# A two-block fp32 model on one core: the second block's causal masks moved from TensorE to VectorE, its factor matmuls spread over more rows, its output gates through tanh, and four pooled tiles held back instead of two

## Chip, core and metric

The kernel runs on one core of one Trainium2 chip. The metric is device time in microseconds (us), from the first to the last instruction; the median of three runs counts.

## The reference, cut to what matters

A first block (dilated attention, convolution, recurrence, feed-forward; width 1024, 1024 tokens) is followed by two layers of a second block over 16 meta tokens and the 1024. The change touches the second block only:

```python
for l in range(2):
    u_pool, z_pool, c_q, c_kv, k_rope, z_mla, g_pool, g_mla = split(rmsnorm(h) @ w_in[l])
    y_pool = (pool_mix(u_pool) * silu(z_pool)) @ pool_w_up[l]
    # 8 heads, q and k of 96, rms-normed per head and token
    s = q @ k.T / sqrt(96);  s = where(key <= query, s, -1e30)
    o = softmax(s) @ v
    y_mla = (o * silu(z_mla)) @ mla_w_up[l]
    merged = sigmoid(g_pool) * y_pool + sigmoid(g_mla) * y_mla
    h = h + merged @ w_out[l]
```

## The kernel before

Everything lies transposed, channels on the 128 partitions and tokens along a row (L2 = 1040). Each fp32 operand is split into a high and a low part, and each product is three matmuls (`mm3`, lines 125 to 127: wh by xh, wh by xl, wl by xh). A row of tokens is cut into chunks: 352, 344, 344 in layer 0, 512 and 512 in layer 1, whose last layer leaves the meta tokens out. A framework schedules the program when it is built: each engine executes its own fixed list in order and waits on semaphores for the others.

Per layer, `attn2` is the middle of the work. For each of eight heads `prep` multiplies q and k by their norm factors: `frh` holds the factors as rows (high parts in rows 0 to 24, low parts in 32 to 56), and a matmul with the selector `esel` (`fp`, line 1535) repeats them over the head's rows. Then it finds each query's largest score: a matmul per query tile of 128 and key chunk of up to 512 (`mx`, line 1552); where the tile's diagonal lies in the chunk, a second matmul adds a bf16 mask through the identity (line 1554); VectorE reduces the bank to a column (line 1555). The negated maxima go into row 96 of q.

The scores proper stand transposed, keys on partitions: `st` (lines 1592 to 1594), on the diagonal again a mask matmul (line 1596), then exp on ScalarE (line 1602), its high part `ph` (1605 or 1607), its low part `pl` (1608) and three matmuls into `ob` (1624 to 1626). `run` issues score tile i and, `LAG` = 3 tiles later, its `ob`. There are 18 score tiles a head in layer 0 and 14 in layer 1. Three PSUM banks rotate for `st`, five for the other products.

Since a head's chain passes through three engines, `run` mixes in other matmuls from `fill`: first the 16 tiles of the two output gates, stored to DRAM, then the eight pooled tiles `mp` (from `th` and `tl`, the split pooled input, line 1291), each multiplied by its gate `gp` (line 1282). `units` counts the pieces of fill and `keep` of them are not handed out before the end of the last head; the rest of `fill` follows at the end of `run`.

At the end the sums `lcol` of the softmax are inverted and copied by DMA into rows of `rh` (high parts from row 0, low parts from row 32; `rlgrp`), and a matmul with the selector `ep` (`rb`, line 1490, in `om_pair`) repeats them over the heads' rows. The last head pair's three (two in layer 1) `rb` can only come after the last `ob`. Then the attention tiles `oh`, `ol` go through `mla_w_up` and are merged under the second gate `gm` (lines 1407 to 1415).

Of the kernel before, what the change touches and what calls it, by code (L numbers as in the profile page):

```python
# [11 lines left out]
F32R = mybir.dt.float32r  # L12
BF = mybir.dt.bfloat16
# [33 lines left out]
def f(t):  # L47
    return t.bitcast(F32)


class B:
# [1010 lines left out]
    def layer(self, l):  # L1062
# [190 lines left out]
        def fill():  # L1253
            for dst, m0 in ((self.gpd[l], 21), (self.gmd[l], 29)):
                for m in range(8):
                    wh, wl = self.w(win[m0 + m])
                    t = self.d("gt")
                    for c0, n in CM:
                        ps = self.mmb()
                        for k in range(8):  # L1260
                            self.mm3(ps[:, :n], [(wh[:, wk(k)], wl[:, wk(k)], xh[k][:, c0:c0 + n], xl[k][:, c0:c0 + n])],
                                     first=k == 0, last=k == 7)
                            if k == 7:
                                nc.vector.tensor_tensor(t[:, c0:c0 + n], ps[:, :n], zs[:, c0:c0 + n], op=OP.mult)
                                if c0 + n == L2:
                                    nc.sync.dma_start(dst[m][:, M0:], t[:, M0:])
                            yield
            for g in range(4):
                t = self.d("tr")
                nc.sync.dma_start(t[:, M0:], self.td[l][g][:, M0:])  # L1270
                h, lo = self.ur("th"), self.ur("tl")
                nc.vector.tensor_copy(h[:, M0:], t[:, M0:])
                nc.vector.tensor_tensor(lo[:, M0:], t[:, M0:], f(h[:, M0:]), op=OP.subtract)
                th.append(h)
                tl.append(lo)
            for m in range(8):
                if m % 2 == 0:
                    wh, wl = self.w(self.i[f"pu_{l}"][m // 2])
                off = 512 * (m % 2)
                t = self.d("gp")  # L1280
                nc.sync.dma_start(t[:, M0:], self.gpd[l][m][:, M0:])
                nc.scalar.activation(t[:, M0:], t[:, M0:], AF.Sigmoid)
                y = mp[m] = self.u("mp")
                for c0, n in CM:
                    ps = self.mmb()
                    for k in range(4):
                        wk4 = slice(off + 128 * k, off + 128 * k + 128)
                        self.mm3(ps[:, :n], [(wh[:, wk4], wl[:, wk4], th[k][:, c0:c0 + n], tl[k][:, c0:c0 + n])],
                                 first=k == 0, last=k == 3)
                        if k == 3:  # L1290
                            nc.vector.tensor_tensor(y[:, c0:c0 + n], ps[:, :n], t[:, c0:c0 + n], op=OP.mult)
                        yield

        silu_gate(17, self.zd[l][0])
# [26 lines left out]
            else:  # L1321
                nc.sync.dma_start(self.qnd[l][m][:, M0:], t[:, M0:])

        fr = self.ur("frh", (57, L2))
        nc.gpsimd.memset(f(fr[0:57, :]), 0.0)

        def qstats():
            if HSD & 1:
                yield YD
            hs.add(0)  # L1330
            if HSD & 2:
                yield YD
            headinv(hs.done(), aq, 16, False)
            for _ in range(HS2):
                yield YD
            for g in range(3):
                ps = self.axb("fr")
                part = T2[4 * g:4 * g + 4]
                for q, (c0, n) in enumerate(part):
                    nc.tensor.transpose(ps[0:25, 128 * q:128 * q + n], FR[:n, 4 * g + q, :], self.ident[:n, :n])  # L1340
                c0 = part[0][0]
                wd = part[-1][0] + part[-1][1] - c0
                nc.scalar.activation(fr[0:25, c0:c0 + wd], ps[0:25, :wd], AF.Copy)
                nc.vector.tensor_tensor(fr[32:57, c0:c0 + wd], ps[0:25, :wd], f(fr[0:25, c0:c0 + wd]), op=OP.subtract)
            yield YD

        att = self.attn2(l, fr, fill())
# [53 lines left out]
        for m in range(8):  # L1401
            if m % 2 == 0:
                wh, wl = self.w(self.i[f"mu_{l}"][m // 2])
            off = 512 * (m % 2)
            t = self.d("gm")
            nc.sync.dma_start(t[:, M0:], self.gmd[l][m][:, M0:])
            nc.scalar.activation(t[:, M0:], t[:, M0:], AF.Sigmoid)
            h, lo = self.ur("gh"), self.ur("gl")
            gh.append(h)
            gl.append(lo)  # L1410
            y = mp[m]

            def ev(ci, c0, n, ps, t=t, y=y, h=h, lo=lo):
                nc.vector.tensor_tensor(t[:, c0:c0 + n], ps, t[:, c0:c0 + n], op=OP.mult)
                nc.vector.tensor_tensor(y[:, c0:c0 + n], y[:, c0:c0 + n], t[:, c0:c0 + n], op=OP.add)
                nc.scalar.activation(h[:, c0:c0 + n], y[:, c0:c0 + n], AF.Copy)
                if late:
                    late.pop(0)()
                late.append(lambda: nc.vector.tensor_tensor(lo[:, c0:c0 + n], y[:, c0:c0 + n], f(h[:, c0:c0 + n]), op=OP.subtract))
            (self.projk if m == 0 else self.proj)(wh, wl, lambda k: slice(off + 128 * k, off + 128 * k + 128), oh, ol, CM, ev)  # L1420
# [38 lines left out]
    def rlgrp(self, l, h0, h1):  # L1459
# [8 lines left out]
        nc.vector.tensor_copy(rlh[R, :nl], rl[R, :nl])  # L1468
        nc.vector.tensor_tensor(rll[R, :nl], rl[R, :nl], f(rlh[R, :nl]), op=OP.subtract)
        rh = self.rh  # L1470
        for q, t in ((0, rlh), (32, rll)):
            for h in range(h0, h1):
                nc.sync.dma_start(f(rh[q + h:q + h + 1, M0:]).rearrange("o (a b) -> o a b", a=16), f(t[16 * h:16 * h + 16, :nl]))

# [24 lines left out]
    def attn2(self, l, fr, fill):  # L1499
# [7 lines left out]
        HT, VT = {}, {}  # L1507
        self.lcol = self.tiny("lcol", (P, 65))
        self.oh, self.ol = [], []
        self.rh = self.ur("rh", (40, L2))  # L1510
        nc.gpsimd.memset(f(self.rh[0:40, :]), 0.0)

        def prep(hd):
            qf, kf = self.d("qf", (96, L2)), self.d("kf", (97, L2))
# [30 lines left out]
            for i, (q0, n) in enumerate(QT):  # L1545
                ke = q0 + n
                for ci, k0 in enumerate(range(0, ke, 512)):
# [1 line left out]
                    ps = self.mmb("mx")  # L1549
                    dg = max(k0, q0)  # L1550
                    has = dg < k1
                    nc.tensor.matmul(ps[:n, :k1 - k0], qh[0:96, q0:q0 + n], kh[0:96, k0:k1], start=True, stop=not has)  # L1552
                    if has:
                        nc.tensor.matmul(ps[:n, dg - k0:k1 - k0], self.idb[:n, :n], self.mk[:n, 1, dg - q0:k1 - q0], start=False, stop=True)  # L1554
                    nc.vector.tensor_reduce(mxp[:n, i, ci:ci + 1], ps[:n, :k1 - k0], axis=AX, op=OP.max)  # L1555
                    yield
            mx = self.tiny("mx2", (P, NT2))
            nc.vector.tensor_reduce(mx, mxp, axis=AX, op=OP.max, negate=True)
# [23 lines left out]
        def s_part(hd, c0, n, j, lastj):  # L1582
# [8 lines left out]
            diag = d1 > s0 and s0 < 128 * j + kn  # L1591
            mms = [lambda: nc.tensor.matmul(st[:kn, :w], kh[0:97, ksl], qh[0:97, s0:c1], start=True, stop=False),  # L1592
                   lambda: nc.tensor.matmul(st[:kn, :w], kh[0:96, ksl], ql[0:96, s0:c1], start=False, stop=False),  # L1593
                   lambda: nc.tensor.matmul(st[:kn, :w], kl[0:96, ksl], qh[0:96, s0:c1], start=False, stop=not diag)]  # L1594
            if diag:
                mms.append(lambda: nc.tensor.matmul(st[:kn, 0:d1 - s0], self.idb[:kn, :kn], self.mk[:kn, 0, s0 - 128 * j:d1 - 128 * j],  # L1596
                                                    start=False, stop=True))

            def evac():
                p = self.s("p")  # L1600
                ph, pl = self.sr("ph"), self.sr("pl")
                nc.scalar.activation(p[:kn, :w], st[:kn, :w], AF.Exp, scale=SC)  # L1602
                state["i"] = i = state.get("i", -1) + 1
                if i % PHD < PHA:
# [37 lines left out]

        def run():
            units = 16 * len(CQ0) * 8 + 8 * len(CQ0) * 4
            keep = 2 * len(CQ0) * 4
            done = 0
            pend = []
            gen = None
# [64 lines left out]
    def b2_consts(self):  # L1713
# [2 lines left out]
        bof = self.tiny("bof", (P, 63))  # L1716
        nc.sync.dma_start(bof, self.i["bo"])
        nc.vector.tensor_copy(self.bo, bof.rearrange("p (a b) -> p a b", a=7))
        self.esel = self.c2p.tile(list((57, 16, 97)), F32R, name="esel")
        ef = self.u("ef", (57, 1024))  # L1720
        nc.sync.dma_start(ef[:, :776], self.i["esel"][:, 0:776])
        nc.vector.tensor_copy(self.esel[:, 0:8, :], ef[:, :776].rearrange("p (a b) -> p a b", a=8))
        ef = self.u("ef", (57, 1024))
        nc.sync.dma_start(ef[:, :776], self.i["esel"][:, 776:1552])
        nc.vector.tensor_copy(self.esel[:, 8:16, :], ef[:, :776].rearrange("p (a b) -> p a b", a=8))
        self.ep = self.c2p.tile(list((40, 4, P)), F32R, name="ep")
        ef = self.u("ef", (40, 512))
        nc.sync.dma_start(ef, self.i["ep"])
        nc.vector.tensor_copy(self.ep, ef.rearrange("p (a b) -> p a b", a=4))

# [8 lines left out]
def _consts():  # L1739
# [39 lines left out]
    bk = np.zeros((128, 9), np.float32)  # L1779
    bk[:32, 8] = 1.0  # L1780
    bo = np.concatenate([bo, bk[:, None]], 1)
    esel = np.zeros((57, 16, 97), np.float32)
    for h in range(8):
        esel[h, h, :64] = 1.0
        esel[8 + h, h, 64:96] = 1.0
        esel[24, h, 96] = 1.0
        esel[16 + h, 8 + h, :96] = 1.0
    esel[32:56] = esel[0:24]
    ep = np.zeros((40, 4, 128), np.float32)
    for m in range(4):  # L1790
        ep[2 * m, m, :64] = 1.0
        ep[2 * m + 1, m, 64:] = 1.0
    ep[32:40] = ep[0:8]
    ic = np.ones((4, 16), np.float32)
    for g in range(4):
        w = 2 << g
        cnt = np.minimum(np.arange(1, 17), w).astype(np.float32)
        ic[g] = np.float32(w) / cnt
    icnt = np.tile(ic.reshape(1, 64), (128, 1))
    return dict(bo=bo.reshape(128, 63), esel=esel.reshape(57, 1552), ep=ep.reshape(40, 512), icnt=icnt, cst=cst, qp=qp, sel1=sel1, e2=e2, mask=mask.reshape(128, 384))  # L1800


def _layout(x):
# [102 lines left out]
```

## Time and profile before

| | |
|---|---|
| median of three runs | 2974.47 us (2971.53 to 2975.08) |
| profiled execution | 2971.57 us, its span 2969.8 us |
| TensorE matmul busy | 2893.7 us, 97% |
| VectorE busy | 1707.3 us, 57% |
| ScalarE busy | 973.8 us, 33% |
| granted TensorE clock | 0.984 of full |

Busy time of TensorE counts from a matmul's start to its modelled end, and matmuls overlap: 97% says that there is nearly always one under way, not how densely they follow each other. That is read from the distance between their starts.

### The profile page before, as it was taken

The numbers are of one execution on the slowest core, as the hardware profiler recorded it, in microseconds if no ns is written. First come the engines' busy times: TensorE is split into PE (matmuls) and PEld (weight loads), VectorE is DVE, ScalarE is ACT, GpSimd is POOL, SyncE is SP. The second block draws the span as 40 slices with busy tenths as digits, with TensorE's granted clock in tenths as the row PEclk, the third lists the DMA queues.
The fourth block names the chain that finished last, engine by engine and source line by source line (L and its number), as shares of the span: only waits on it lengthen the run. The fifth ranks groups of instructions, "written<-read, shape, count | busy, mean of one in ns | idle before, by whom it ended". The sixth has DMA issues, their size and how long they took to land.

```text
span 2969.8 us, 37159 instructions
## 1 busy us (share of the span) xinstructions
PE 2893.7 (97%) x14918; PEld 2442.2 (82%) x14918; DVE 1707.3 (57%) x2940; ACT 973.8 (33%) x1617; POOL 33.7 (1%) x101
## 2 busy tenths in 40 slices
PE   8979999999999999999999999989999999999999
PEld 6857788888888888899899998879978887777677
DVE  6986766544545546544665665564534665656562
ACT  4143432111111124433234343743432223433630
POOL 1000000000000000000000000000000000000000
PEclk9989999999999999999999999989999999999999
DMA  3111212111111111524223232532313323232542
GB/s 129 54 36 64 86 59 69 46 50 50 43 50 50 43 47 53 174 62 125 65 83 91 76 101 59 187 112 105 123 54 98 116 75 91 88 85 74 177 141 76
DMA packets 93520, 249.93 MB, mean 84 GB/s; under 512 B 29489, under 2 KB 30786, under 8 KB 93348
## 3 DMA queue, kind: packets, MB, share of 16 engines
q1 hardware_dynamic: 93348, 247.56, 26.3%
q8 instruction: 117, 1.92, 0.3%
q14 instruction: 55, 0.45, 0.0%
HBM read 182.86 MB, written 60.06 MB: 82 GB/s over the span
## 4 chain that ended last, share of the span: by engine, by line
PE 93%; DVE 4%; ACT 1%; DMA 1%; issue 0%; SPq 0%; POOL 0%; DVEq 0%; ACTq 0%; POOLq 0%
PE mm L125 27%; PE mm L127 26%; PE mm L126 26%; PE mx L1552 1%; PE st L1593 1%; PE st L1594 1%; PE st L1592 1%; PE ob L1624 1%; PE ob L1626 1%; PE ob L1625 1%; PE fp L1535 1%; PE cs L230 1%; PE mxp L720 0%; PE mx L1554 0%; PE st L1596 0%
## 5 line engine op out<-in xcount | busy, mean ns | idle before, releaser
L125 PE MATMUL mm<-xh,wh 128*128 128x512 f32 (+2 forms) x2352 | 879.0, 375 | 25.7 <-DVE kf L772 10.9
L127 PE MATMUL mm<-xh,wl 128*128 128x512 f32 (+2 forms) x2352 | 855.5, 364 | 0.2 <-POOL wl L118 0.2
L126 PE MATMUL mm<-xl,wh 128*128 128x512 f32 (+2 forms) x2352 | 854.3, 364 | 0.0
L125 PEld LDWEIGHTS mm<-xh,wh 128*128 128x128 f32 x2352 | 448.4, 191 | 91.1 <-DVE kf L772 12.5
L127 PEld LDWEIGHTS mm<-xh,wl 128*128 128x128 f32 x2352 | 445.6, 189 | 58.1 <-issue 0.7
L126 PEld LDWEIGHTS mm<-xl,wh 128*128 128x128 f32 x2352 | 447.2, 190 | 52.8 <-issue 0.9
L117 ACT ACTIVATE wh<-wr 128x1024 fp32r<-128x1024 f32 (+2 forms) x217 | 221.9, 1023 | 811.6 <-PE mm L126 627.4
L118 DVE TENSOR_TENSOR wl<-wr,wh 128x1024 fp32r<-128x1024 f32 (+2 forms) x215 | 253.3, 1178 | 122.2 <-ACT wh L117 121.4
L1602 ACT ACTIVATE p<-st 128x272 f32<-128x272 f32 (+8 forms) x256 | 106.1, 414 | 325.7 <-PE st L1596 179.1
L127 PE MATMUL mm<-fh,wl 128*128 128x512 f32 x512 | 201.5, 394 | 0.0
L126 PE MATMUL mm<-fl,wh 128*128 128x512 f32 x512 | 201.1, 393 | 0.0
L125 PE MATMUL mm<-fh,wh 128*128 128x512 f32 x512 | 201.1, 393 | 0.0
L1608 DVE TENSOR_TENSOR pl<-p,ph 128x272 fp32r<-128x272 f32 (+8 forms) x256 | 118.1, 462 | 143.5 <-ACT ph L1605 140.2
L655 DVE TENSOR_TENSOR x<-mm,x 128x512 f32<-128x512 f32 x208 | 142.3, 690 | 97.3 <-PE mm L127 96.9
L625 DVE SCALAR_TENSOR_TENSOR ft<-mm,zs 128x512 f32<-128x512 f32 x64 | 44.1, 691 | 166.3 <-PE mm L127 164.9
L1555 DVE TENSOR_REDUCE mxp<-mx 128x1 f32<-128x512 f32 (+9 forms) x232 | 116.6, 522 | 38.6 <-PE mx L1552 22.2
L126 PEld LDWEIGHTS mm<-fl,wh 128*128 128x128 f32 x512 | 96.2, 188 | 22.4
L125 PEld LDWEIGHTS mm<-fh,wh 128*128 128x128 f32 x512 | 96.1, 188 | 22.2
L127 PEld LDWEIGHTS mm<-fh,wl 128*128 128x128 f32 x512 | 96.1, 188 | 21.8
L127 PE MATMUL mm<-gh,wl 128*128 128x512 f32 (+2 forms) x320 | 112.2, 351 | 0.0
L126 PE MATMUL mm<-gl,wh 128*128 128x512 f32 (+2 forms) x320 | 112.2, 350 | 0.0
L125 PE MATMUL mm<-gh,wh 128*128 128x512 f32 (+2 forms) x320 | 111.9, 350 | 0.0
(437 smaller groups left out, 4600.7 us busy)
## 6 DMA issues: line engine op xcount, KB each, us to landing
wr<-in_w_in SPq DMA_DIRECT2D x91, 512.0 KB
wr<-in_w_up SPq DMA_DIRECT2D x32, 512.0 KB
wr<-in_w_down SPq DMA_DIRECT2D x26, 512.0 KB
wr<-in_wo SPq DMA_DIRECT2D x16, 512.0 KB
wr<-in_wq SPq DMA_DIRECT2D x12, 384.0 KB
hd<-hr SPq DMA_DIRECT2D x8, 520.0 KB
kd<-kn SPq DMA_DIRECT2D x8, 520.0 KB
kf<-kd SPq DMA_DIRECT2D x16, 260.0 KB
```

The costliest lines, as they stand in the source:

```text
L117: nc.scalar.activation(hi[:, :width], raw[:, :width], AF.Copy)
L118: self.loe.tensor_tensor(lo[:, :width], raw[:, :width], f(hi[:, :width]), op=OP.subtract)
L125: nc.tensor.matmul(ps, wh, xh, start=first and q == 0, stop=False)
L126: nc.tensor.matmul(ps, wh, xl, start=False, stop=False)
L127: nc.tensor.matmul(ps, wl, xh, start=False, stop=last and q == n - 1)
L230: ins = self.nc.tensor.matmul(ps[:n, j:j + 1], acc[:nrows, c0:c0 + n], self.ones[:nrows, :], start=True, stop=True)
L625: nc.vector.scalar_tensor_tensor(t, ps, 0.0, zs[:, c0:c0 + n], op0=OP.max, op1=OP.mult)
L655: nc.vector.tensor_tensor(x[:, c0:c0 + n], ps, x[:, c0:c0 + n], op=OP.add)
L1535: nc.tensor.matmul(ps[0:R, :n], self.esel[:, e, 0:R], fr[:, c0:c0 + n], start=True, stop=True)
L1555: nc.vector.tensor_reduce(mxp[:n, i, ci:ci + 1], ps[:n, :k1 - k0], axis=AX, op=OP.max)
L1602: nc.scalar.activation(p[:kn, :w], st[:kn, :w], AF.Exp, scale=SC)
L1608: nc.vector.tensor_tensor(pl[:kn, :w], p[:kn, :w], f(ph[:kn, :w]), op=OP.subtract)
```

## The change

Five edits, all in the second block.

- The 152 mask matmuls on the score tiles become 152 additions of the mask on VectorE, in place in PSUM, ahead of the exp.
- The 152 mask matmuls on the maxima go; the reduction there becomes one VectorE instruction that adds a mask (`mz`: 512 columns of zero and the 128 of the triangle) and takes the maximum, followed by a small one that reads the result out. Key chunks without a diagonal keep the plain reduction.
- The low parts in `frh` begin at row 64 instead of 32, so `fp` contracts over 89 rows instead of 57; those in `rh` likewise, so `rb` contracts over 72 instead of 40.
- Both gates use sigmoid(x) = (1 + tanh(x/2))/2. The halves are folded into `th` (now made on ScalarE with a scale, line 1272) and into `ep`; the multiplication by the gate becomes (gate + 1) times product, one instruction as before. In the built program 40 loads of ScalarE's function tables in the second block become four.
- `keep` is doubled: four pooled tiles remain for the end of the attention instead of two.

```diff
-                nc.vector.tensor_copy(h[:, M0:], t[:, M0:])
-                nc.vector.tensor_tensor(lo[:, M0:], t[:, M0:], f(h[:, M0:]), op=OP.subtract)
+                nc.scalar.activation(h[:, M0:], t[:, M0:], AF.Copy, scale=0.5)
+                nc.vector.scalar_tensor_tensor(lo[:, M0:], t[:, M0:], 0.5, f(h[:, M0:]), op0=OP.mult, op1=OP.subtract)
...
-                nc.scalar.activation(t[:, M0:], t[:, M0:], AF.Sigmoid)
+                nc.scalar.activation(t[:, M0:], t[:, M0:], AF.Tanh, scale=0.5)
...
-                            nc.vector.tensor_tensor(y[:, c0:c0 + n], ps[:, :n], t[:, c0:c0 + n], op=OP.mult)
+                            nc.vector.scalar_tensor_tensor(y[:, c0:c0 + n], t[:, c0:c0 + n], 1.0, ps[:, :n], op0=OP.add, op1=OP.mult)
...
-        fr = self.ur("frh", (57, L2))
+        fr = self.ur("frh", (89, L2))
...
-                nc.vector.tensor_tensor(fr[32:57, c0:c0 + wd], ps[0:25, :wd], f(fr[0:25, c0:c0 + wd]), op=OP.subtract)
+                nc.vector.tensor_tensor(fr[64:89, c0:c0 + wd], ps[0:25, :wd], f(fr[0:25, c0:c0 + wd]), op=OP.subtract)
...
-        for q, t in ((0, rlh), (32, rll)):
+        for q, t in ((0, rlh), (64, rll)):
...
-                    nc.tensor.matmul(ps[:n, :k1 - k0], qh[0:96, q0:q0 + n], kh[0:96, k0:k1], start=True, stop=not has)
+                    nc.tensor.matmul(ps[:n, :k1 - k0], qh[0:96, q0:q0 + n], kh[0:96, k0:k1], start=True, stop=True)
                     if has:
-                        nc.tensor.matmul(ps[:n, dg - k0:k1 - k0], self.idb[:n, :n], self.mk[:n, 1, dg - q0:k1 - q0], start=False, stop=True)
-                    nc.vector.tensor_reduce(mxp[:n, i, ci:ci + 1], ps[:n, :k1 - k0], axis=AX, op=OP.max)
+                        z0 = 512 + k0 - q0
+                        nc.vector.tensor_tensor_reduce(ps[:n, :k1 - k0], ps[:n, :k1 - k0], self.mz[:n, z0:z0 + k1 - k0], 1.0, -3.0e38,
+                                                       OP.add, OP.max, mxp[:n, i, ci:ci + 1])
+                    else:
+                        nc.vector.tensor_reduce(mxp[:n, i, ci:ci + 1], ps[:n, :k1 - k0], axis=AX, op=OP.max)
...
-            if diag:
-                mms.append(lambda: nc.tensor.matmul(st[:kn, 0:d1 - s0], self.idb[:kn, :kn], self.mk[:kn, 0, s0 - 128 * j:d1 - 128 * j],
-                                                    start=False, stop=True))
...
+                if diag:
+                    nc.vector.tensor_tensor(st[:kn, 0:d1 - s0], st[:kn, 0:d1 - s0], self.mk[:kn, 0, s0 - 128 * j:d1 - 128 * j], op=OP.add)
                 nc.scalar.activation(p[:kn, :w], st[:kn, :w], AF.Exp, scale=SC)
...
-            keep = 2 * len(CQ0) * 4
+            keep = 4 * len(CQ0) * 4
```

TensorE's list before, at a diagonal tile of the maxima in layer 0 (`mm` is fill, `ob` the output product, `mx` the maxima):

```order
L1626 MATMUL ob_12659<-pl_12666,vh_11885 65x384
L1552 MATMUL mx_12765<-kh_12454,qh_12452 128x384
L1554 LDWEIGHTS idb
L1554 MATMUL mx_12765<-mk,idb 128x128
L125 MATMUL mm_12776<-xh_7403,wh_12771 128x352
```

The same place in the changed program:

```order
L1628 MATMUL ob_11490<-pl_11496,vh_10546 65x384
L1552 MATMUL mx_11600<-kh_11310,qh_11308 128x384
L125 MATMUL mm_11565<-xh_7707,wh_11560 128x352
L126 MATMUL mm_11565<-xl_7708,wh_11560 128x352
```

The mask and the load of its identity are gone, and fill follows the maxima directly.

TensorE's list before, at the end of layer 0's attention, from the last fill to the first product of the attention tiles:

```order
L127 MATMUL mm_16014<-th_15224,wl_15910 128x344
L1624 MATMUL ob_15755<-ph_15836,vh_14772 65x272
L1625 MATMUL ob_15755<-ph_15836,vl_14773 65x272
L1626 MATMUL ob_15755<-pl_15837,vh_14772 65x272
L1624 MATMUL ob_15755<-ph_15861,vh_14772 65x144
L1625 MATMUL ob_15755<-ph_15861,vl_14773 65x144
L1626 MATMUL ob_15755<-pl_15862,vh_14772 65x144
L1624 MATMUL ob_15755<-ph_15885,vh_14772 65x16
L1625 MATMUL ob_15755<-ph_15885,vl_14773 65x16
L1626 MATMUL ob_15755<-pl_15886,vh_14772 65x16
L1490 MATMUL rb_16030<-rh_10269,ep 128x352
```

And in the changed program, around the last `ob` and then at the first of the last `rb` (the first of 126 matmuls of fill between them, and the last, are shown):

```order
L1628 MATMUL ob_15591<-pl_15697,vh_14645 65x144
L125 MATMUL mm_15770<-th_15246,wh_15742 128x344
L1626 MATMUL ob_15591<-ph_15721,vh_14645 65x16
L1627 MATMUL ob_15591<-ph_15721,vl_14646 65x16
L1628 MATMUL ob_15591<-pl_15722,vh_14645 65x16
L125 MATMUL mm_15770<-th_15258,wh_15742 128x344
...
L127 MATMUL mm_15945<-th_15264,wl_15864 128x344
L1490 MATMUL rb_15961<-rh_10272,ep 128x352
```

Before, nothing stood between the last nine `ob` and the `rb`; now there is fill between the `ob`, and 126 matmuls of it (78 in layer 1) ahead of the `rb`.

VectorE's list before, in one head of layer 0 (`pl` the low part of the exp, `gt` an eviction of fill):

```order
L1608 TENSOR_TENSOR pl_13277<-p_13275,ph_13276 128x256
L1555 TENSOR_REDUCE mxp_13131<-mx_13290 128x1
L1555 TENSOR_REDUCE mxp_13131<-mx_13293 128x1
L1608 TENSOR_TENSOR pl_13307<-p_13305,ph_13306 128x128
L1555 TENSOR_REDUCE mxp_13131<-mx_13320 128x1
```

And in the changed program, such a place in one head (line 1603 adds the mask, ISA is the new instruction and its read-out):

```order
L1603 TENSOR_TENSOR st_13190<-st_13190,mk 128x128
L1264 TENSOR_TENSOR gt_13040<-mm_13129,zs 128x344
L1610 TENSOR_TENSOR pl_13196<-p_13194,ph_13195 128x256
L1558 TENSOR_REDUCE mxp_13069<-mx_13212 128x1
L1555 ISA mx_13215,mxp_13069<-mx_13215,mz 128x256
L1555 ISA mxp_13069 128x1
L1603 TENSOR_TENSOR st_13221<-st_13221,mk 128x128
L1610 TENSOR_TENSOR pl_13227<-p_13225,ph_13226 128x128
```

The additions have entered VectorE's list between the `pl` of older tiles, and one reduction of two became a pair.

## Rows read from the trace of the kernel before

**Rows 1.** Windows: stretch, length, then PE, PEld, DVE, ACT, POOL busy, PEclk, DMA.

```profile
1530.00:1855.00 325.00, 324.27 (x2122) 295.56 (x2122) 201.18 (x436) 131.61 (x311) 1.73 (x19) 1.00 0.28 81
2442.00:2750.00 308.00, 307.64 (x1544) 232.81 (x1542) 177.12 (x347) 116.46 (x238) 1.55 (x17) 1.00 0.28 81
```

**Rows 2.** Timeline of PE around a mask: start, length, engine, line, instruction.

```profile
1601.98 0.33 PE L1626 MATMUL ob<-pl,vh 128*65 128x384 f32 x1
1602.16 0.33 PE L1552 MATMUL mx<-kh,qh 96*128 96x384 f32 x1
1602.34 0.23 PE L1554 MATMUL mx<-mk,idb 128*128 128x128 bf16 x1
1602.38 0.40 PE L125 MATMUL mm<-xh,wh 128*128 128x344 f32 x1
1602.62 0.32 PE L126 MATMUL mm<-xl,wh 128*128 128x344 f32 x1
```

**Rows 3.** Timeline of PE around a matmul over 57 rows.

```profile
1826.07 0.32 PE L126 MATMUL mm<-xl,wh 128*128 128x344 f32 x1
1826.22 0.32 PE L127 MATMUL mm<-xh,wl 128*128 128x344 f32 x1
1826.48 0.41 PE L1535 MATMUL fp<-frh,esel 57*96 57x384 f32 x1
1826.82 0.44 PE L1592 MATMUL st<-qh,kh 97*128 97x384 f32 x1
1827.10 0.34 PE L1593 MATMUL st<-ql,kh 96*128 96x384 f32 x1
```

**Rows 4.** Timeline of PE in the first block, around two matmuls over 97 rows.

```profile
389.27 0.40 PE L125 MATMUL mm<-mh,wh 128*128 128x512 f32 x1
389.51 0.63 PE L941 MATMUL rb<-rh,e 97*128 97x512 f32 x2
389.97 0.40 PE L126 MATMUL mm<-ml,wh 128*128 128x512 f32 x1
```

**Rows 5.** Timeline, end of layer 0's attention; in brackets idle time before.

```profile
1938.40 1.28 ACT L1602 ACT_TABLE_LOAD   x1
...
1940.17 0.27 PE L1624 MATMUL ob<-ph,vh 16*65 16x16 f32 x1 [3.74 <-ACT ph L1605]
...
1947.45 1.20 PE L1490 MATMUL rb<-rh,ep 40*128 40x352 f32 x3 [6.79 <-DMA rh<-rll]
```

**Rows 6.** Windows: that end, and the stretch at half clock that overlaps it.

```profile
1931.00:1948.00 17.00, 3.40 (x17) 2.23 (x16) 4.07 (x9) 9.01 (x13) 0.49 (x5) 0.65 0.31 86
1936.10:1953.20 17.10, 6.57 (x23) 5.93 (x24) 3.92 (x11) 7.96 (x11) 0.49 (x5) 0.50 0.27 77
```

**Rows 7.** Timeline, end of layer 1's attention.

```profile
2830.02 0.92 PE L1490 MATMUL rb<-rh,ep 40*128 40x512 f32 x2 [2.58 <-DMA rh<-rll]
```

**Rows 8.** Groups of the second block by line and shape: busy us, mean ns, idle before.

```profile
L1555 DVE TENSOR_REDUCE mxp<-mx 128x1 f32<-128x512 f32 x96 | 64.4, 686 | 21.7 <-PE mx L1552 18.6 <-PE mx L1554 2.9
L1264 DVE TENSOR_TENSOR gt<-mm,zs 128x512 f32<-128x512 f32 x32 | 22.0, 687 | 17.9 <-PE mm L127 17.6
L1264 DVE TENSOR_TENSOR gt<-mm,zs 128x344 f32<-128x344 f32 x32 | 16.4, 511 | 10.5 <-PE mm L127 10.3
```

**Rows 9.** Line 1558: the smallest reductions; duration ns min/median/max.

```profile
L1558 DVE TENSOR_REDUCE mx<-mxp x16: 174/182/184, 1465.9 to 2749.1; 128x9 f32<-128x27 f32 x16
```

**Rows 10.** Timeline: one score tile of layer 0, from its exp to its last use.

```profile
1702.97 0.40 ACT L1602 ACTIVATE p<-st 128x272 f32<-128x272 f32 x1 [2.35 <-PE st L1594]
...
1703.86 0.44 DVE L1608 TENSOR_TENSOR pl<-p,ph 128x272 fp32r<-128x272 f32 x1 [0.81 <-ACT ph L1605]
...
1711.52 0.29 PE L1626 MATMUL ob<-pl,vh 128*65 128x272 f32 x1
```

**Rows 11.** The page, part 5: a product from PSUM with a constant in it.

```profile
L625 DVE SCALAR_TENSOR_TENSOR ft<-mm,zs 128x512 f32<-128x512 f32 x64 | 44.1, 691 | 166.3 <-PE mm L127 164.9 <-ACT zs L253 1.4
```

**Rows 12.** Timeline: the first pooled tile of layer 1 waits for its input.

```profile
2759.98 0.79 PE L125 MATMUL mm<-th,wh 128*128 128x512 f32 x1 [4.84 <-DVE th L1272]
```

More of the change, by code (lines that the diff above doesn't have):

```diff
@@ L1322, in layer @@
                 nc.sync.dma_start(self.qnd[l][m][:, M0:], t[:, M0:])
-        fr = self.ur("frh", (57, L2))
-        nc.gpsimd.memset(f(fr[0:57, :]), 0.0)
+        fr = self.ur("frh", (89, L2))
+        nc.gpsimd.memset(f(fr[0:89, :]), 0.0)
         def qstats():
@@ L1406, in layer @@
             nc.sync.dma_start(t[:, M0:], self.gmd[l][m][:, M0:])
-            nc.scalar.activation(t[:, M0:], t[:, M0:], AF.Sigmoid)
+            nc.scalar.activation(t[:, M0:], t[:, M0:], AF.Tanh, scale=0.5)
             h, lo = self.ur("gh"), self.ur("gl")
@@ L1413, in ev @@
             def ev(ci, c0, n, ps, t=t, y=y, h=h, lo=lo):
-                nc.vector.tensor_tensor(t[:, c0:c0 + n], ps, t[:, c0:c0 + n], op=OP.mult)
+                nc.vector.scalar_tensor_tensor(t[:, c0:c0 + n], t[:, c0:c0 + n], 1.0, ps, op0=OP.add, op1=OP.mult)
                 nc.vector.tensor_tensor(y[:, c0:c0 + n], y[:, c0:c0 + n], t[:, c0:c0 + n], op=OP.add)
@@ L1509, in attn2 @@
         self.oh, self.ol = [], []
-        self.rh = self.ur("rh", (40, L2))
-        nc.gpsimd.memset(f(self.rh[0:40, :]), 0.0)
+        self.rh = self.ur("rh", (72, L2))
+        nc.gpsimd.memset(f(self.rh[0:72, :]), 0.0)
         def prep(hd):
@@ L1593, in s_part @@
                    lambda: nc.tensor.matmul(st[:kn, :w], kh[0:96, ksl], ql[0:96, s0:c1], start=False, stop=False),
-                   lambda: nc.tensor.matmul(st[:kn, :w], kl[0:96, ksl], qh[0:96, s0:c1], start=False, stop=not diag)]
-            if diag:
-                mms.append(lambda: nc.tensor.matmul(st[:kn, 0:d1 - s0], self.idb[:kn, :kn], self.mk[:kn, 0, s0 - 128 * j:d1 - 128 * j],
-                                                    start=False, stop=True))
+                   lambda: nc.tensor.matmul(st[:kn, :w], kl[0:96, ksl], qh[0:96, s0:c1], start=False, stop=True)]
             def evac():
@@ L1718, in b2_consts @@
         nc.vector.tensor_copy(self.bo, bof.rearrange("p (a b) -> p a b", a=7))
-        self.esel = self.c2p.tile(list((57, 16, 97)), F32R, name="esel")
-        ef = self.u("ef", (57, 1024))
+        self.esel = self.c2p.tile(list((89, 16, 97)), F32R, name="esel")
+        ef = self.u("ef", (89, 1024))
         nc.sync.dma_start(ef[:, :776], self.i["esel"][:, 0:776])
         nc.vector.tensor_copy(self.esel[:, 0:8, :], ef[:, :776].rearrange("p (a b) -> p a b", a=8))
-        ef = self.u("ef", (57, 1024))
+        ef = self.u("ef", (89, 1024))
         nc.sync.dma_start(ef[:, :776], self.i["esel"][:, 776:1552])
         nc.vector.tensor_copy(self.esel[:, 8:16, :], ef[:, :776].rearrange("p (a b) -> p a b", a=8))
-        self.ep = self.c2p.tile(list((40, 4, P)), F32R, name="ep")
-        ef = self.u("ef", (40, 512))
+        self.mz = self.c2p.tile([P, 640], BF, name="mz")
+        nc.gpsimd.memset(self.mz[:, 0:512], 0.0)
+        nc.vector.tensor_copy(self.mz[:, 512:640], self.mk[:, 1, :])
+        self.ep = self.c2p.tile(list((72, 4, P)), F32R, name="ep")
+        ef = self.u("ef", (72, 512))
         nc.sync.dma_start(ef, self.i["ep"])
@@ L1781, in _consts @@
     bo = np.concatenate([bo, bk[:, None]], 1)
-    esel = np.zeros((57, 16, 97), np.float32)
+    esel = np.zeros((89, 16, 97), np.float32)
     for h in range(8):
@@ L1787, in _consts @@
         esel[16 + h, 8 + h, :96] = 1.0
-    esel[32:56] = esel[0:24]
-    ep = np.zeros((40, 4, 128), np.float32)
+    esel[64:88] = esel[0:24]
+    ep = np.zeros((72, 4, 128), np.float32)
     for m in range(4):
-        ep[2 * m, m, :64] = 1.0
-        ep[2 * m + 1, m, 64:] = 1.0
-    ep[32:40] = ep[0:8]
+        ep[2 * m, m, :64] = 0.5
+        ep[2 * m + 1, m, 64:] = 0.5
+    ep[64:72] = ep[0:8]
     ic = np.ones((4, 16), np.float32)
@@ L1799, in _consts @@
     icnt = np.tile(ic.reshape(1, 64), (128, 1))
-    return dict(bo=bo.reshape(128, 63), esel=esel.reshape(57, 1552), ep=ep.reshape(40, 512), icnt=icnt, cst=cst, qp=qp, sel1=sel1, e2=e2, mask=mask.reshape(128, 384))
+    return dict(bo=bo.reshape(128, 63), esel=esel.reshape(89, 1552), ep=ep.reshape(72, 512), icnt=icnt, cst=cst, qp=qp, sel1=sel1, e2=e2, mask=mask.reshape(128, 384))
 def _layout(x):
```

## The prediction

> **What bounds the kernel now.** I read the granted clock first (0.984 of full in the mean, so nearly all matmuls go at the upper level, 2.4 GHz), then the busy time by stretch, then the timeline of TensorE, and the waits last. In the main loops of the two attentions TensorE is busy in 324.27 of 325.00 us and in 307.64 of 308.00, VectorE in 201.18 and 177.12, ScalarE in 131.61 and 116.46 [rows 1]. So TensorE sets the time there, and whatever is taken out of its stream comes off the span, as long as VectorE (62% and 58%) stays behind it. Busy time doesn't say what an instruction costs in that stream, since matmuls overlap. The distance between starts does, and all prices below are such distances. The second place is the end of layer 0's attention, where TensorE is busy in 3.40 of 17.00 us [rows 6]. There it waits first for the exp of the last score tiles, behind a load of ScalarE's tables, and then 6.79 us for the copies into `rh` [rows 5].
>
> **The masks on TensorE.** A matmul of 384 columns is followed after 0.18 us (1601.98 to 1602.16) by the next [rows 2]; one of 344 columns after 0.15 (1826.07 to 1826.22) [rows 3]. From the start of `mx` at 1602.16 to the second matmul of fill at 1602.62 pass 0.46 us; without the mask they would be 0.18 + 0.15 = 0.33. So the mask takes 0.13 us out of the stream: 0.04 between its start and that of the next matmul, and the rest by delaying the one after (0.24 from 1602.38 to 1602.62 where 0.15 is usual). The changed program has 152 + 152 = 304 fewer of them. 304 x 0.13 = 39.5 us. Bounds: 0.04 each is 12 us, if the delay behind it returned without the mask; 0.23, the length of the row itself, is 70 us. I take 0.13, which is the whole distance in a dense stretch.
>
> **The factor matmuls.** Rows 1826.22 to 1827.10 hold a matmul of 344 columns, one over 57 rows of 384 columns, and one of 384: 0.15 + 0.18 + 0.18 = 0.51 us expected, 0.88 there, so 0.37 too long [rows 3]. The control is in the first block: one matmul of 512 columns and two over 97 rows take 389.27 to 389.97, 0.70 us or 0.23 each, with nothing on top [rows 4]. So it is the row count, or something that goes with it. Rows that follow each other without another matmul between them pay once: counted in TensorE's list of before, the 88 `fp` stand in 45 such visits and the 20 `rb` in 17. The last visit of each layer's `rb` waits for a DMA and is counted with the ends; that leaves 60. I give `rb`, over 40 rows, the price of `fp`. 60 x 0.37 = 22.2 us. The new counts, 89 and 72, were never run here; score matmuls over 96 rows stand in the same stream as those over 97 (lines 1592 and 1593), and I take 72 to behave like them. Bounds: nothing, and 22.2.
>
> The Trainium skill has a rule against this edit. "TensorE: Matmul & The Clock Gate", section "Why this matters for your kernels", says that a single matmul over 32 rows takes as long as one over 128, and that a gain comes only from running several side by side. By that the edit is worth 0 and not 22.2 us. "TensorEngine Tiling (Array Packing)", section "Key Properties", says that changing the tiling mode drains the engine; the 0.37 us at entry and exit agree with that one.
>
> **The ends of the attentions.** Layer 0: 17.00 - 3.40 = 13.6 us idle [rows 6]. With it the clock fell to half: of the 17.10 us at half clock TensorE was busy in 6.57 [rows 6], which would have taken half, 3.3. Layer 1: 2.58 us [rows 7]. Together 19.5 us. In the changed program 126 and 78 matmuls of fill stand between the last `ob` and the last `rb`. At 0.15 for 344 columns [rows 3] and 0.23 for 512 [rows 4], they last 19 and 18 us. The chain that they have to cover is, from the last `ob` at 1940.17 to `rb` at 1947.45, 7.3 us [rows 5]. So it is covered more than twice over. This fill is no new work: it is taken out of the main loop, where it would otherwise have filled TensorE. The loop is left with 5% less fill (24 more of 480 pieces kept back in layer 0). If the loop then lacked cover, this would return as idle time there; the slack below says that it doesn't. The table loads go too (1.28 us each [rows 5]); they cost time only at this end, so I count nothing more for them.
>
> **What VectorE gets.** Score masks: 687 ns for 512 columns, 511 for 344 [rows 8] is 1.05 ns a column, so about 0.29 us for 128; 152 of them. Maxima: no row shows the new instruction. From below, it does what a reduction (686) and a two-operand instruction (687) [rows 8] each do in one pass, so no more than now, plus a read-out, for which the smallest reduction, 0.18 us [rows 9], is nearest. From above, it takes as long as both after each other, 0.69 more at 512 columns. I take the lower end, since it reads one bank and one mask as an addition does. Layer 0 has 72 masks of each kind, nine a head, and I take seven of its eight heads, 63, for the stretch of 325 us (layer 1: 80 and 70). VectorE goes to 201.18 + 63 x (0.29 + 0.18) = 231 us, while TensorE's stretch shrinks to some 325 - 16 - 8 = 301 (126 masks, half of the 45 visits): 77%. At the upper end 63 x 0.69 = 43 more, 274 us, still below.
>
> That is cover in bulk; for the single tile, an exp that ends at 1703.37 gives a `pl` that ends at 1704.30, and the `ob` that needs it starts at 1711.52 [rows 10]. The mask adds a hop, 0.29 us and a place in VectorE's queue, whose instructions take 0.5 to 0.7 there [rows 8], to a path with 7.2 us to spare. So nothing is charged to the loop. Where there is no cover is `prep` of each layer's first head, in which VectorE's reductions set the pace: I allow 3 us for both layers, for read-outs and for masks there whose removal gives nothing. Gates with a constant cost what the plain product does (691 [rows 11] against 687 [rows 8]). `th` moves to ScalarE; TensorE waits for it now 4.84 us in layer 1 [rows 12], and I expect the same within a microsecond or two.
>
> **The sum**, against the profiled execution: 2971.57 - 39.5 - 22.2 - 19.5 + 3 = 2893.4 us. It lies 2.9 us below the median of the runs, 2974.47, so I add half of that: **2895 us**.
>
> **Rivals.**
> - *The delay behind the mask stays.* The next weights would still have to be loaded in a short time, and a mask is worth only its 0.04 us: 2895 + 27.5 = 2922. For it: the 0.24 stands behind the mask, not in it. Against: behind `ob` and fill of the same widths no such gap follows [rows 2].
> - *Row count does nothing.* 57 rows cost because of what surrounds them (a wait, PSUM): 2895 + 22 = 2917. Against it is the control [rows 4], though that is one place in another block. The skill's equal-time rule ends here.
> - *The ends stay.* The kept fill lacks inputs (its gates arrive late through DMA) or the loop becomes thin: 2895 + 19.5 = 2915.
> - *VectorE becomes the bound*, which ends on the other side. It needs the new instruction to run far off the rows, at several passes. It decides from (301 - 231) / 63 = 1.1 us above the reduction's time on the average masked tile, and loses against before from (325 - 231) / 63 = 1.5. At 2 us above, layer 0's stretch takes 231 + 126 = 357 us, 32 more than before, and layer 1's 177 + 70 x 2.47 = 350, 42 more: 2972 + 74 - 19.5 = 3026. For it: an operation that this kernel has never run, writing its result back to PSUM. Against: both halves of it run at one column per 1.05 ns [rows 8].
>
> **Chances.** My sum, 2872 to 2908: 0.60. Masks worth their slot alone, about 2922: 0.13. Rows nothing, 2917: 0.07. Ends nothing, 2915: 0.06. Two of these together or VectorE half in the way, 2928 to 2965: 0.05. More than the sum (below 2872, masks towards their upper bound): 0.02. No change: 0.03. Slower through VectorE: 0.04. From 2872 to 2927 lie 0.86 of it; that is the range. What a measurement of this kernel can tell from no change is 0.2%, 6 us: faster 0.93, same 0.03, slower 0.04.
>
> **What would show it.** In the profile after: `mx` followed by fill at the distance of its columns, then 0.15 to the next; `fp` over 89 rows without a gap on either side; no idle time of TensorE ahead of the last `rb` of either layer, and no half-clock stretch behind it; the two loops shorter by some 20 to 25 us each with VectorE at about three quarters; the new instruction with 512 columns near 0.69 us. I am wrong if VectorE's share there nears 1, if TensorE waits for `ph`, `pl` or the exp inside the loops, or if the 0.24 behind `mx` is still there.

## The result, and the profile after

The changed kernel takes **2928.27 us** (median of 4 runs, 2924.73 to 2929.47), the kernel before 2973.47 beside it: ratio 0.9846, 95% interval 0.9829 to 0.9863. So it is faster, by 45 us, where 79 were forecast; the range ended at 2927, 1.3 us short of it. The profiled execution has a span of 2927.2 us at a granted clock of 0.982.

The two main loops, by windows, as in [rows 1]. Columns: stretch, length, then PE, PEld, DVE, ACT, POOL busy, PEclk, DMA.

```profile
1546.00:1850.00 304.00, 299.92 (x1967) 286.80 (x1966) 214.66 (x562) 134.76 (x318) 1.73 (x19) 0.99 0.30 86
2424.00:2725.00 301.00, 296.62 (x1436) 235.91 (x1434) 193.79 (x480) 121.17 (x247) 1.55 (x17) 0.98 0.29 85
```

VectorE is at 71% and 64% of the two stretches, below the 77% worked out for the first. But TensorE, which had 0.73 and 0.36 us idle in [rows 1], now has 4.1 and 4.4, and its clock isn't full any more.

TensorE's timeline in a dense stretch of layer 0, answering to [rows 2] and [rows 3]: a row-maxima matmul, and a factor matmul over 89 rows.

```profile
1612.94 0.34 PE L1552 MATMUL mx<-kh,qh 96*128 96x384 f32 x1
1613.12 0.32 PE L125 MATMUL mm<-xh,wh 128*128 128x344 f32 x1
1613.28 0.31 PE L126 MATMUL mm<-xl,wh 128*128 128x344 f32 x1
```

```profile
1589.65 0.34 PE L1535 MATMUL fp<-frh,esel 89*97 89x344 f32 x1
1589.83 0.32 PE L125 MATMUL mm<-xh,wh 128*128 128x344 f32 x1
1589.99 0.32 PE L126 MATMUL mm<-xl,wh 128*128 128x344 f32 x1
```

Both follow the forecast: 0.18 and 0.16 us, the distances of plain matmuls; the 0.24 behind `mx` is gone, and so is nearly all of the 0.37 around `fp`.

The end of layer 0's attention, answering to [rows 5]: the last `rb` waits for nothing. Between the last `ob` (1908.43) and it stand 126 matmuls of fill.

```profile
1928.48 0.32 PE L127 MATMUL mm<-th,wl 128*128 128x344 f32 x1
1928.64 0.64 PE L1490 MATMUL rb<-rh,ep 72*128 72x352 f32 x3
```

What was not forecast stands in three other places. First, the loads of the wider selector, cut from the view by tile (duration in ns, start in us):

```profile
L1726 SPq DMA_DIRECT2D ef<-in_esel x1: 3188/3188/3188, 1161.8 to 1161.8; - x1
L1733 SPq DMA_DIRECT2D ef<-in_ep x1: 10069/10069/10069, 1165.1 to 1165.1; - x1
L1724 DVE CAST esel<-ef x1: 561/561/561, 1175.7 to 1175.7; 89x776 fp32r<-89x776 f32 x1
L1727 DVE CAST esel<-ef x1: 561/561/561, 1186.8 to 1186.8; 89x776 fp32r<-89x776 f32 x1
```

In the kernel before, these casts started at 1167.5 and 1169.7. VectorE works in order, and behind the second cast stand the evictions of the key path and the chain of a norm that ends in `zc`; TensorE needs `zc` next, and its timeline shows what that costs:

```profile
1196.13 2.15 PE L248 MATMUL bc<-ident,zc 128*128 128x128 f32 x9 [13.34 <-DVE zc L1048]
```

The first factor matmul of layer 0 is 17 us later than before (1456.1 against 1439.1). Second, the row-maxima matmuls, by source line, in the kernel before and then after (TensorE's idle time before them by releaser; weight loads and matmuls are both counted, so the time is about twice the gap):

```profile
  ACT qh L1537: 3.0, 7
```

```profile
its engine sat idle before it (us, times) until:
  ACT qh L1537: 15.7, 15
```

Seven of the 14 heads that are prepared inside the loops begin their row maxima with such a wait: the first `mx` starts 0.87 to 1.68 us later than the columns before it need. Together these waits are 8.4 us; in the kernel before there were two, of 1.4 us together. Third, cut from the timeline of VectorE, ScalarE and TensorE at the start of layer 0's last head:

```profile
1861.29 1.23 DVE L118 TENSOR_TENSOR wl<-wr,wh 128x1024 fp32r<-128x1024 f32 x1 [0.42 <-ACT wh L117]
1862.43 0.43 DVE L1634 TENSOR_TENSOR osb<-osb,zt 64x272 f32<-64x272 f32 x1
1862.78 0.48 DVE L1603 TENSOR_TENSOR st<-st,mk 128x128 f32<-128x128 f32 x2
1863.16 0.49 ACT L1604 ACTIVATE p<-st 128x384 f32<-128x384 f32 x1 [1.62 <-DVE st L1603]
1863.70 0.44 PE L1595 MATMUL st<-qh,kh 97*128 97x384 f32 x1 [1.74 <-ACT p L1604]
```

The score tile was complete at 1861.3. Its mask stands in VectorE's queue behind a weight split of 1.23 us, the exp behind the mask, and TensorE behind the exp, for its bank. This wait is new, but it is hardly a cost: right behind it TensorE waits again, for the pooled input `th`, and `th` waits for a DMA. The chain of work that ended last goes through that DMA there and not through the mask (start, length, what):

```profile
1861.28 4.67 DMA tr<-td
...
1865.97 1.08 ACT th L1272
...
1867.09 0.95 PE mm L125 x2
```

A balance of TensorE over both attentions, from the first `fp` to the last `rb` of each layer. *Stream* is the sum of the distances between the starts of matmuls; where a distance is more than 0.33 us over its columns at 2.4 GHz, the rest is a *wait*; of stretches at half clock, what goes beyond their columns at 2.4 GHz is *lost*. Which matmuls at the ends of such a stretch belong to it is a matter of counting, and moves several us (20 in one row) between the two columns; their sum is firm, and only it is used below. Each balance is of one profiled execution, the last column the median of all; that of the score masks undone is of an execution of 2933.0 us, 5.6 below its median.

| kernel | stream | waits | lost at half clock | sum | time, us |
|---|---|---|---|---|---|
| before | 942.6 | 21.9 | 20.2 | 984.7 | 2973.5 |
| after | 889.3 | 19.8 | 19.8 | 928.9 | 2928.3 |
| 96-row selector | 889.8 | 22.8 | 15.6 | 928.3 | 2913.4 |
| row counts undone | 907.5 | 16.8 | 18.4 | 942.8 | 2926.6 |
| maxima masks undone | 905.1 | 22.4 | 13.0 | 940.4 | 2941.8 |
| score masks undone | 909.3 | 18.4 | 6.8 | 934.5 | 2938.6 |
| all masks undone | 924.0 | 17.5 | 13.1 | 954.6 | 2955.3 |
| both end edits undone | 892.0 | 38.8 | 17.7 | 948.6 | 2954.2 |
| interleaved, empty steps | 890.0 | 12.9 | 12.7 | 915.7 | 2901.1 |
| the same, two tiles kept | 890.9 | 16.7 | 5.0 | 912.8 | 2898.0 |

### The profile page after: what moved, and what is told of

Same layout as the page of the kernel before. It is cut to its first block, busy times and chain, and to the rows that moved or that the text cites. A ratio compares the mean times of both kernels' runs of the same rounds, so it can differ in the third digit from the quotient of the medians.

```text
span 2927.2 us, 36718 instructions
## 1 busy us (share of the span) xinstructions
PE 2846.9 (97%) x14614; PEld 2439.1 (83%) x14614; DVE 1735.7 (59%) x3237; ACT 936.1 (32%) x1588; POOL 34.2 (1%) x102
## 4 chain that ended last, share of the span: by engine, by line
PE 92%; DVE 4%; DMA 1%; ACT 1%; issue 1%; SPq 0%; POOL 0%; DVEq 0%; ACTq 0%; POOLq 0%
PE mm L125 27%; PE mm L127 26%; PE mm L126 26%; PE mx L1552 1%; PE ob L1626 1%; PE ob L1628 1%; PE ob L1627 1%; PE st L1596 1%; PE st L1597 1%; PE st L1595 1%; DMA ef<-in_esel 1%; PE cs L230 1%; PE mxp L720 0%; PE fp L1535 0%; DMA tr<-td 0%
## 5 line engine op out<-in xcount | busy, mean ns | idle before, releaser
L125 PE MATMUL mm<-xh,wh 128*128 128x512 f32 (+2 forms) x2352 | 866.0, 369 | 26.6 <-DVE kf L772 10.9
L125 PEld LDWEIGHTS mm<-xh,wh 128*128 128x128 f32 x2352 | 447.1, 190 | 89.9 <-DVE kf L772 12.5
L126 PEld LDWEIGHTS mm<-fl,wh 128*128 128x128 f32 x512 | 96.2, 188 | 22.4
L1607 ACT ACTIVATE ph<-p 128x272 fp32r<-128x272 f32 (+8 forms) x206 | 92.6, 450 | 11.5 <-PE ob L1627 4.1
```

The costliest lines, as they stand in the source:

```text
L125: nc.tensor.matmul(ps, wh, xh, start=first and q == 0, stop=False)
L126: nc.tensor.matmul(ps, wh, xl, start=False, stop=False)
L1607: nc.scalar.activation(ph[:kn, :w], p[:kn, :w], AF.Copy)
```

## The experiments

The theory after the result: masks and factor matmuls are worth about what was forecast on TensorE; the gain is missing because the selector's load holds VectorE up (some 17 us) and because masks in VectorE's queue make TensorE wait inside the loops (some 17 with the half clock). The rival: the prices themselves were too high. All times are against runs of the kernel before on the same chip.

**The selector's load.** First 96 rows, then 97 rows, nothing else:

```diff
-        self.esel = self.c2p.tile(list((89, 16, 97)), F32R, name="esel")
-        ef = self.u("ef", (89, 1024))
+        self.esel = self.c2p.tile(list((96, 16, 97)), F32R, name="esel")
+        ef = self.u("ef", (96, 1024))
```

> The changed kernel with the selector constant padded from 89 to 96 rows (tile, staging buffer and loads; the factor matmuls still read rows 0 to 88). Theory: the 89-row loads run on a single DMA engine (178 packets of 3104 bytes one after another, 0.128 us each, over 22 us; 57 rows before: 114 packets in 4.5 us), and VectorE's in-order queue holds the key path of layer 0 behind their casts. A row count that 16 divides takes that away: casts near 1167 and 1170 us, first factor matmul of layer 0 near 1437 instead of 1454 us, total about 2911 (2908 to 2914). Rival: it is the bytes or the casts themselves that cost; then 96 rows are as slow as 89 or slower, 2928 to 2930.

> The changed kernel with the selector padded to 97 rows, a number without divisors like 89. If the number of DMA engines follows from the divisors of the row count, the two loads run on one engine again: 194 packets of 0.128 us in a row, second cast near 1188 to 1190 us, total 2928 to 2931. If the cure in the 96-row run was the padding as such (or an even time slot), the casts stay near 1167 and 1168 and the total near 2913.

Measured: 2913.42 us for 96 rows (ratio 0.9796, 0.9781 to 0.9811), 2928.39 for 97 in one run. The casts with 96 rows, then with 97, by tile:

```profile
L1724 DVE CAST esel<-ef x1: 560/560/560, 1166.9 to 1166.9; 96x776 fp32r<-96x776 f32 x1
L1727 DVE CAST esel<-ef x1: 559/559/559, 1168.1 to 1168.1; 96x776 fp32r<-96x776 f32 x1
```

```profile
L1724 DVE CAST esel<-ef x1: 565/565/565, 1176.9 to 1176.9; 97x776 fp32r<-97x776 f32 x1
L1727 DVE CAST esel<-ef x1: 566/566/566, 1189.0 to 1189.0; 97x776 fp32r<-97x776 f32 x1
```

So neither bytes nor casts cost, but the row count: one row more than 96 brings everything back. It is 14.9 us (2928.3 - 2913.4). In the changed kernel the 178 packets of 3104 bytes, 0.128 us each, lie one after another over 22 us; in the kernel before, 114 of 0.123 us (14.0 us in sum) lay within 4.6 us, three side by side. The Trainium skill, "DMA: Bandwidth & Descriptors", section "🔬 Why a DMA increments its semaphore by 16 and not by 1", says that a DMA is split over the largest number of engines, up to 16, that divides its outermost dimension. By that 57 rows use 3, 89 and 97 one, 96 sixteen. The traces agree for the first three (97 rows: 194 packets one after another over 24 us); for 96 rows they show 192 packets, 28.6 us in sum, within 2.5 us, eleven side by side on average, which fits sixteen and doesn't prove it.

**The row counts undone** (57 and 40 rows everywhere, the old selectors):

```diff
-        fr = self.ur("frh", (89, L2))
+        fr = self.ur("frh", (57, L2))
-        for q, t in ((0, rlh), (64, rll)):
+        for q, t in ((0, rlh), (32, rll)):
```

> The changed kernel with the row counts undone (factor rows 57 and 40, low halves from row 32, selectors 57 and 40 rows); masks on VectorE, tanh gates and kept tiles stay. By the prediction's term the factor matmuls lose 60 visits x 0.37 = 22 us again, and the selector load gives 17 back: 2928 + 22 - 17 = 2933 (2927 to 2938). Rival (the row count does nothing for the matmuls, only the load counts): 2911. If, beside that, longer factor matmuls take the waits of TensorE in front of the row-maxima matmuls away, up to 8 us less than the 2933.

Measured: 2926.64 us (0.9839, 0.9824 to 0.9853). The stream grows by 18.2 us, 0.30 for each of some 60 visits, so the row count does act on the matmuls; the rival that it does nothing is out. Against the kernel with the 96-row selector, from which little but the matmuls differs, the time is 13.2 us longer. But with its own selector the row edit as a whole was worth nothing: 2926.6 without it, 2928.3 with it.

**The masks**, each half and then all back on TensorE:

```diff
-                        nc.vector.tensor_tensor_reduce(ps[:n, :k1 - k0], ...
+                        nc.tensor.matmul(ps[:n, dg - k0:k1 - k0], self.idb[:n, :n], ...
+                    nc.vector.tensor_reduce(mxp[:n, i, ci:ci + 1], ps[:n, :k1 - k0], axis=AX, op=OP.max)
```

> The changed kernel with only the 152 masks of the row maxima back on TensorE (plain maximum reduction on VectorE); score masks stay on VectorE. By the term 152 x 0.13 = 20 us slower: 2948. If the new waits of TensorE in front of the row-maxima matmuls (some 11 us, and about 9 more lost to the half clock behind them) come from the combined add-and-maximum on VectorE, they go, and the time is 2928 to 2935; if they come from the score masks or from TensorE arriving sooner, they stay and it is 2945 to 2950.

```diff
+                mms.append(lambda: nc.tensor.matmul(st[:kn, 0:d1 - s0], self.idb[:kn, :kn], ...
-                    nc.vector.tensor_tensor(st[:kn, 0:d1 - s0], st[:kn, 0:d1 - s0], ...
```

> The changed kernel with only the 152 masks of the score tiles back on TensorE; the row maxima keep the combined add-and-maximum on VectorE. By the term 152 x 0.13 = 20 us slower: 2948. If the waits in front of the row-maxima matmuls come from the score masks added on VectorE (they delay the factor products and, through the exponential, ScalarE's copies of them), those waits go and it is 2928 to 2935; if not, 2945 to 2950.

> The changed kernel with all 304 masks back on TensorE. One half gave 13.5 us, the other 10.3; if they add up, 2952 (2948 to 2956). By the term of the prediction alone (304 x 0.13 = 39.5) it would be 2968; if the two halves share the waits that they cost on VectorE, so that undoing both frees more than the sum, 2940 to 2947.

Measured: 2941.80 (0.9889, 0.9874 to 0.9903), 2938.60 (0.9882, 0.9866 to 0.9899) and 2955.31 us (0.9942, 0.9929 to 0.9956). The halves are worth 13.5 and 10.3, together 27.0. On the stream they are worth more: 15.8, 20.0 and 34.7 us, that is 0.10, 0.13 and 0.114 a mask. The difference is given back on TensorE as waits and half clock: with the score masks on TensorE these are 25.2 us in place of 39.6 (in an execution that was 5.6 us faster than its median, so this difference is too large), with the maxima masks there 35.4, with both 30.6. So neither clean outcome of the expectations came: with the score masks back on TensorE the waits shrink but don't go. The idle time before the maxima, by source line, with the score masks back (15.7 after, and 15.7 with the maxima masks back):

```profile
  ACT qh L1537: 8.7, 11
```

The waits of the first `mx` over the columns before it, 8.4 us after, are 8.4 with the maxima masks back and 4.4 with the score masks or all masks back. So 4.0 us of them come from the score masks on VectorE and nothing from the new instruction. Why the other 4.4 are more than the 1.4 of the kernel before isn't shown; that TensorE arrives sooner is one reading. The wait for a score bank at the start of the last heads (1.96 and 1.53 us over the columns) is gone with the score masks back, but the wait for `th` has grown in its place:

```profile
1868.89 0.59 PE L125 MATMUL mm<-th,wh 128*128 128x352 f32 x2 [3.38 <-ACT th L1272]
```

From the last head's first score matmul to this one pass 7.1 us in layer 0 and 6.3 in layer 1, and 6.6 in either layer after: the masks cost nothing to speak of at this place.

**The ends**: two kept tiles, the sigmoid, and both.

```diff
-            keep = 4 * len(CQ0) * 4
+            keep = 2 * len(CQ0) * 4
-            nc.scalar.activation(t[:, M0:], t[:, M0:], AF.Tanh, scale=0.5)
+            nc.scalar.activation(t[:, M0:], t[:, M0:], AF.Sigmoid)
```

> The changed kernel with two pooled tiles kept for the end of each attention instead of four; tanh gates, masks and row counts stay. The prediction put 19.5 us on the two ends of the attentions for the kept tiles and the table loads together. If the kept tiles do it, the idle time in front of the last factor broadcasts comes back with its half-clock stretch: 2940 to 2948. If the gates' table loads did it, 2928 to 2931.

> The changed kernel with the gates through the sigmoid again (ScalarE loads function tables at each change between exponential and sigmoid; broadcast constant 1.0 instead of 0.5), four tiles kept. If the kept tiles alone fill the ends: 2928 to 2932. If the table loads in ScalarE's in-order queue were what was late at the ends: 2936 to 2948.

> The changed kernel with both edits at the ends of the attentions undone: sigmoid gates and two kept tiles. Each of them alone changed nothing (2925 and 2927 against 2928). Theory: either one is enough to cover the end, so only together do they bring back the idle time in front of the last factor broadcasts and its half-clock stretch, as the prediction's 19.5 us: 2944 to 2951. Rival: the masks and rows had already taken the end waits away; then 2925 to 2931.

Measured: 2925.09 (0.9837, 0.9823 to 0.9850), 2926.52 (0.9843, 0.9829 to 0.9856) and 2954.21 us (0.9934, 0.9922 to 0.9947). Neither edit alone is worth anything, both together 26 us. With both undone, the end of layer 0 looks as in [rows 5], cut from the timeline:

```profile
1926.38 1.28 ACT L1604 ACT_TABLE_LOAD   x1
1927.68 0.29 ACT L1604 ACTIVATE p<-st 128x144 f32<-128x144 f32 x1
1928.01 1.28 ACT L1407 ACT_TABLE_LOAD   x1
1929.30 1.07 ACT L1407 ACTIVATE gm<-gm 128x1040 f32<-128x1040 f32 x1
1930.28 0.31 ACT L1607 ACTIVATE ph<-p 128x144 fp32r<-128x144 f32 x1
...
1930.64 0.38 PE L1626 MATMUL ob<-ph,vh 128*65 128x144 f32 x1 [4.35 <-ACT ph L1607]
...
1939.66 0.92 PE L1490 MATMUL rb<-rh,ep 72*128 72x352 f32 x2 [6.80 <-DMA rh<-rll]
```

A gate's table load and sigmoid stand between an exp and the copy of its result, and then nothing covers the DMAs to `rh`. How many fill matmuls stand between the last `ob` and the next `rb` in the two layers explains the rest: 0 and 18 before, 0 and 0 with both undone, 54 and 30 with two tiles and tanh (8.8 and 7.3 us), 98 and 33 with four and sigmoid, 126 and 78 after. The chain to be covered takes about 7 us, so the last three kernels cover it in both layers and the first two don't: without the table loads the last `ob` comes early enough for the two tiles to last.

**The waits before the maxima**, attacked by the order of the factor products, then by two empty steps, then with two kept tiles, all on the 96-row selector (the last also with `keep = 2 * len(CQ0) * 4`):

```diff
+            kq = [[(kf, kh, kl, hd, *c) for c in CHF], [(qf, qh, ql, 8 + hd, *c) for c in CQ]]
+            kq = [x[i] for i in range(3) for x in kq if i < len(x)]
...
+            yield
+            yield
             mxp = self.tiny("mxp", (P, NT2, 3))
...
-                    cost = [0.1 * FPC] * (len(CHF) + len(CQ)) + [1] * (nmx + 4)
+                    cost = [0.1 * FPC] * (len(CHF) + len(CQ)) + [1] * (nmx + 6)
```

> The kernel with the 96-row selector (2913.4), and each head's factor products in the order key 0, query 0, key 1, query 1, key 2, query 2 instead of all keys first, so that the copies which the first row-maxima matmul reads are made four products earlier. Theory: the eight waits in front of that matmul (8.9 us) and the half-clock stretches that follow some of them (about 7 us lost) go, nothing else changes: 2899 to 2906. Rival: VectorE's and ScalarE's queues are late as a whole by the masks, so the wait only moves to the next matmul that needs a copy: 2911 to 2915.

> The kernel with the 96-row selector and interleaved factor products (2909.9), with two empty steps of the head's preparation between the factor products and the first row-maxima matmul (20 or so fill matmuls more between them in layer 0). Theory: the copies are then ready in layer 0 too, the three waits (4.0 us) and the half-clock stretches behind them go: 2902 to 2907. Rival: VectorE and ScalarE are late by a steady amount, and TensorE waits at the same instructions: 2909 to 2912.

> The same with two kept tiles instead of four (tanh gates stay). Two kept tiles alone were 3 us faster than four; if that adds up: 2899 to 2905. If the fill matmuls moved into the heads only shift where TensorE waits: 2902 to 2909.

Measured: 2909.86 (0.9787, 0.9774 to 0.9801), 2901.09 (0.9757, 0.9744 to 0.9771) and 2897.98 us (0.9746, 0.9732 to 0.9759). The first is no more than the measurement can tell from the 96-row kernel: of the waits before the maxima the two of layer 0 stay (1.68 us each), those of layer 1 fall from 5.0 to 2.2 us together. With the empty steps they fall to nothing and 1.2, and the time by 8.8 us: the waits were real cost, and a distance in the order removes them. They are 4.4 of the 8.8; the time at half clock within the attentions falls too, from 27.4 to 20.4 us. The last kernel is the fastest of the study, 30 us below the changed one, though its 3 us below the one before it are no more than the measurement can tell. Its loops, by windows:

```profile
1535.00:1840.00 305.00, 303.30 (x2004) 290.16 (x2004) 212.73 (x555) 131.92 (x311) 1.72 (x19) 1.00 0.31 91
2400.00:2690.00 290.00, 289.31 (x1417) 229.84 (x1417) 193.04 (x476) 118.77 (x239) 1.63 (x18) 1.00 0.30 88
```

The granted clock is full again there, with VectorE as busy as in the changed kernel (70% and 67%): it was not VectorE's share that cost, but single tiles that came late.

## Why the prediction failed, by its steps

The direction and the three mechanisms were right; the sum failed, by one term that was missing, one that was put at nothing, and two prices. Against the 2895 us of the sum, the missing term is 14.9 us, the masks gave 12.5 less than was put down, the factor matmuls 9.0 less, and the ends 6.5 more: 29.9 of the 33.3 us by which the time lay above it.

- **Not in the sum: the constants' load.** This is the largest error. The prediction costed the instructions of the loops and none of the set-up, though the change turns 57 and 40 rows into 89 and 72 in three DMA loads and three casts. It cost 14.9 us, shown by the runs with 96 and 97 rows. The chance for rows being worth nothing (2917) stood there for another reason.
- **"So nothing is charged to the loop."** This is the step that failed in the argument. The slack of 7.2 us [rows 10] was that of `ob` behind `pl`; the slack of `mx` for the copies of `qh` was not looked at, and there TensorE waits, 8.4 us in place of 1.4, 4.0 of them by the score masks. Masks gave 27.0 us where the stream gained 34.7. The wait for the exp, which the prediction named as what would refute it, came as well, but ahead of one for `th` that hides it.
- **Masks, 39.5 us**: 34.7 on the stream, 0.114 each in place of 0.13. The rival of 0.04 (12 us) is out; the whole distance was the right reading, from one place that was a little dear.
- **Factor matmuls, 22.2 us**: 18.2 on the stream, 0.30 a visit in place of 0.37, and 13.2 in time. The Trainium skill's equal-time rule ("TensorE: Matmul & The Clock Gate", "Why this matters for your kernels") would have given 0; the stream's 18.2 us decide against it here. Most of them lie in the distances ahead of such matmuls and behind them.
- **Ends, 19.5 us**: 26 in this kernel. The fill covers the chain as forecast. That the table loads "cost time only at this end, so I count nothing more for them" missed that the table loads and the kept tiles do the same work twice over.
- **3 us for `prep` and VectorE**: the wait at the first head's transpose is 4.4 us as before (4.5). The new instruction takes 0.69 us at 512 columns and its read-out 0.14, near the lower bound taken.

By wall time the parts, each undone in the changed kernel, give 27.0 + 13.2 + 26 - 14.9 = 51 us, against 45 measured. They share waits, so they don't add exactly; the streams nearly do (34.7 + 18.2, and 2.7 for the ends, make 55.6 against 53.3). What the half-clock time of one run owes to chance stays open: four executions of the kernel with the score masks undone took 2933.0 to 2940.4 us, at mean granted clocks from 0.985 down to 0.982.

## What to carry to other kernels

Cost the set-up of a change like its loops: a constant whose load has become slow, here by its row count and not by its bytes, holds up all that stands behind its cast in an engine's list. When work is moved to an engine with room, look at every product that this engine has to deliver in time, not only at the tile that is moved; share of time says nothing about a single tile that waits behind a long instruction. And a new wait is a cost only if nothing behind it would have waited as long. Where two edits aim at the same idle time, undo both together before either is called worthless.

## What the hardware showed beyond that

- Two loads of 89 rows ran at some 25 GB/s, and SP's queue stood behind them: the issue of the second and that of the next load took 3.19 and 10.07 us in place of 0.29 and 0.28.
- Waits of one to two microseconds inside a dense stream sometimes cost as much again: after 0.90 us at 2548.8 the clock was granted at half for 3.4 us, until 2552.3; after 1.67 us at 1598.0 it was not.
- Two factor products of 352 columns, one after the other, start 0.24 us apart over 57 rows and 0.16 us over 89, in all 16 places. Those of 384 columns mostly start 0.26 us apart with either count, those of 512 0.23; what makes the difference isn't shown.
